# Attention in a two-layer model: both parts of V in one operand, head norms token by token, forget gate in two passes

## The chip, the cores and the metric

The kernel runs on one core of a Trainium2 chip. The metric is the device time of one execution in microseconds. Five engines work side by side, each through its own instructions in a fixed order: TensorE (PE, whose weight loads have a row of their own in the profile, PEld), VectorE (DVE), ScalarE (ACT), GpSimd (POOL), and SyncE (SP), which issues most of the transfers.

## The reference, cut to what matters

The model has two layers over 512 tokens of width 1024. Layer 0 mixes tokens with a gated linear recurrence, layer 1 with attention that has a forget gate (`fox_mixer`); each layer ends in a feed-forward part that retrieves 16 of 16384 experts per head. The change lies in the attention of layer 1 alone.

```python
def fox_mixer(h, in_w, f_b, q_norm_g, k_norm_g, out_w):
    q, k, v, f_logit, og = jnp.split(h @ in_w, [D, 2 * D, 3 * D, 3 * D + H], axis=-1)
    q = rms_norm(q.reshape(B, S, H, E), q_norm_g)          # 16 heads of 64
    k = rms_norm(k.reshape(B, S, H, E), k_norm_g)
    log_f = jax.nn.log_sigmoid(f_logit + f_b)
    cum = jnp.cumsum(log_f, axis=1)                        # per head
    ...
        s = einsum(q, k) * scale + cum[query] - cum[key]   # causal
        p = jax.nn.softmax(s, axis=-1)
        o = einsum(p, v)
    o = o * jax.nn.sigmoid(og)
    return o @ out_w
```

`rms_norm` multiplies by 1/sqrt(mean of squares + 1e-6) over the 64 entries of a head. `h` is the normed and modulated input; `f_logit` is 16 columns wide, one for each head.

## The kernel before, in words

Everything is computed to nearly float32 from two rounded parts: a tensor x is kept as hi = round(x) and lo = x − hi in the type fp32r, and a product of two such tensors is three matmuls, hi·hi, hi·lo and lo·hi (L428 to L430 in `proj_t`; `split`, L229 and L230, makes the parts, the high one on ScalarE, the low one on VectorE).

The attention stage `fox` first computes V for all heads (`values`, in two halves of 512 columns), and between the halves the forget gate: one projection whose 128 columns hold the 16 gate columns and zeros (24 matmuls of 512 tokens), then log-sigmoid, a running sum `cum`, and eight writes of its parts to the DRAM tensor `cx` by GpSimd's queue. From there rows go into the tiles qx and kx, so that the score product adds cum[query] − cum[key] by itself.

Then come eight head pairs, each 128 rows (two heads of 64, called par 0 and par 1). For one pair:

- `heads_norm` projects q and k (2 × 24 matmuls of 512 tokens, L428 to L430). ScalarE makes the squares `sq` (L1215) and a scaled copy `raw` (L1217). A matmul with `sel` as weights (8 columns wide) streams the squares and sums them by head into `ssq`, 8 rows of 256 tokens (L1219). VectorE scales and inverts them (L1222, L1223), ScalarE takes the square root (L1224), which needs a table of its own, and `split` makes two parts rh and rl. Matmuls with `selT` as weights spread these over the 128 rows into `rsb` (L1233, L1234), and VectorE multiplies (L1235).
- `prepare` makes from them the operands qs, qx, ks and kx (L1262 to L1276), eight copies on ScalarE and four subtractions on VectorE.
- `attend` goes through four query blocks for each head: scores `s` by two matmuls (L1293, L1294), mask and maximum on VectorE, the exponential on ScalarE (L1300), reciprocal and scaling on VectorE, transposes `tp` of the probabilities (L1305), and `split` into pth and ptl. Then the product with V: for each of four key blocks three matmuls into `o`, with weights vh, vh and vl (L1310 to L1312). vh holds both heads of the pair, so half of the 128 output rows is the other head's and is not used. Last, `o` goes into y, for the first two pairs through VectorE together with the output gate (L1314), for the others by a copy on ScalarE (L1316).

The loop in the text prepares pairs 0 and 1 first, and pair j + 2 after pair j's attention. The order on each engine is made by the framework's scheduler ahead of time: it takes the earliest instruction in program order that its own estimate of times holds ready, so projections fill the places where the scores wait. On the chip each engine keeps that order whatever the real times are. `bg.pump` hands out rows of the next modulation (VectorE L195, their loads by GpSimd's queue) between the steps. The last six output gates are projected during the last two pairs. The PSUM tag "n" has one buffer, which ssq and rsb of all pairs share in turn.

## Time and profile before

| | us |
|---|---|
| median of 3 runs | 3116.62 |
| lowest, highest | 3116.06, 3117.3 |
| the profiled execution, its own time | 3118.31 |
| its span in the profile | 3116.5 |
| first ssq matmul to last matmul start of o, within the span | 1596.8 to 1819.3 |

The profile is one execution; the times in its views are microseconds from the start of its span. A group's row gives engine, operation, output and inputs, shapes and count, then busy time, the mean length of one in nanoseconds, and the idle time of the engine before them with what ended it. Ends of matmuls are modelled, starts are recorded. For a matmul "128*8 128x256" means weights of 128 rows and 8 columns, and 256 streamed columns; the input that is named first is the streamed one.

### The profile page before, as it was taken

To read this page: it belongs to the slowest core of one execution; us is meant where nothing else is said; L and a number is where in the kernel's file an instruction comes from. 1 tells how busy PE (TensorE), PEld (TensorE's weight loads), DVE (VectorE), ACT (ScalarE), POOL (GpSimd) and SP (SyncE) were. 2 spreads that over 40 slices of the span, in tenths; PEclk is the share of its full clock that TensorE was granted. 3 is DMA by queue.
4 is the path that set the end of the run, shared out by engine and by line. 5 is a ranking of instruction groups with operands and counts; after the bars stand their busy time and mean duration, and the time that the engine had idled before them with its cause. 6 is when DMAs were issued, how large, how long until landed. Compare 5 with 4: busy or idle time off the path is not lost.

```text
span 3116.5 us, 44537 instructions
## 1 busy us (share of the span) xinstructions
PE 3041.4 (98%) x16192; PEld 2672.8 (86%) x16192; DVE 2559.3 (82%) x5274; ACT 1468.3 (47%) x2131; POOL 958.0 (31%) x846
## 2 busy tenths in 40 slices
PE   7999999999999999999999999999999999999999
PEld 5877899988888888888777778999988888888888
DVE  7876889878988888888579867899869887888786
ACT  5754247873333333333457843267843333333332
POOL 0001430007654245452011003400046444444450
PEclk9999999999999999999999999999999999999999
DMA  7543245779999999998332123346699999999994
GB/s 271 170 173 122 102 152 204 269 296 398 403 381 369 349 366 362 375 355 300 131 120 83 56 105 107 126 159 245 257 370 398 349 362 346 354 344 351 340 330 162
DMA packets 300429, 818.99 MB, mean 263 GB/s; under 512 B 28848, under 2 KB 151728, under 8 KB 271664
## 3 DMA queue, kind: packets, MB, share of 16 engines
q1 hardware_dynamic: 168464, 388.79, 35.0%
q0 software_dynamic: 90272, 324.58, 27.6%
q10 hardware_dynamic: 41472, 102.78, 8.5%
q8 instruction: 127, 2.08, 0.3%
q14 instruction: 94, 0.77, 0.1%
HBM read 735.03 MB, written 81.02 MB: 262 GB/s over the span
## 4 chain that ended last, share of the span: by engine, by line
PE 68%; DVE 12%; DMA 6%; issue 3%; ACT 2%; POOL 1%; DVEq 0%; SPq 0%; POOLq 0%; ACTq 0%
PE vacc L1048 26%; PE pacc L428 10%; PE pacc L430 10%; PE pacc L429 10%; DVE wlo L230 3%; PE gps L909 2%; DMA wraw<-in_l_v_dram 2%; DMA wraw<-in_l_uT_dram 2%; DVE rows L957 1%; DVE ge L820 1%; DMA at<-ascr 1%; PE oacc L470 1%; PE oacc L471 1%; PE oacc L469 1%; DVE pg L933 1%
## 5 line engine op out<-in xcount | busy, mean ns | idle before, releaser
L229 ACT ACTIVATE whi<-wraw 128x1024 fp32r<-128x1024 f32 (+1 forms) x646 | 663.0, 1033 | 611.2 <-PE pacc L429 346.7
L428 PE MATMUL pacc<-hhi,whi 128*128 128x384 f32 (+1 forms) x2616 | 920.9, 352 | 13.1 <-ACT at L1028 6.8
L430 PE MATMUL pacc<-hhi,wlo 128*128 128x384 f32 (+1 forms) x2616 | 915.4, 350 | 7.5 <-DVE wlo L230 7.3
L429 PE MATMUL pacc<-hlo,whi 128*128 128x384 f32 (+1 forms) x2616 | 912.2, 349 | 0.0
L230 DVE TENSOR_TENSOR wlo<-wraw,whi 128x1024 fp32r<-128x1024 f32 (+1 forms) x580 | 699.9, 1211 | 212.3 <-ACT whi L229 204.7
L1048 PE MATMUL vacc<-whi,wl 128*128 128x512 f32 x1536 | 601.0, 391 | 2.3 <-DVE wl L1041 2.3
L1048 PE MATMUL vacc<-wlo,wh 128*128 128x512 f32 x1536 | 600.7, 391 | 0.8 <-DVE wlo L230 0.8
L1048 PE MATMUL vacc<-whi,wh 128*128 128x512 f32 x1536 | 598.2, 389 | 0.3 <-ACT whi L229 0.3
L428 PEld LDWEIGHTS pacc<-hhi,whi 128*128 128x128 f32 x2616 | 492.2, 188 | 45.1 <-ACT at L1028 7.8
L430 PEld LDWEIGHTS pacc<-hhi,wlo 128*128 128x128 f32 x2616 | 491.6, 188 | 36.6 <-DVE wlo L230 12.0
L429 PEld LDWEIGHTS pacc<-hlo,whi 128*128 128x128 f32 x2616 | 492.1, 188 | 28.6 <-issue 1.7
L1038 ACT ACTIVATE wh<-at 128x384 fp32r<-128x384 f32 x256 | 134.1, 525 | 778.4 <-DVE at L1034 489.2
L948 POOL DMA_INDIRECT rows<-in_l_v_dram,ei x256 | 355.6, 1389 | 360.6 <-DVE accg L972 335.5
L948 POOL DMA_INDIRECT rows<-in_l_u_dram,ei x256 | 368.7, 1440 | 263.4 <-DVE rows L957 208.9
L1048 PEld LDWEIGHTS vacc<-whi,wl 128*128 128x128 f32 x1536 | 288.7, 188 | 63.4 <-DVE wl L1041 2.6
L1048 PEld LDWEIGHTS vacc<-wlo,wh 128*128 128x128 f32 x1536 | 288.7, 188 | 58.7 <-DVE wlo L230 1.1
L1048 PEld LDWEIGHTS vacc<-whi,wh 128*128 128x128 f32 x1536 | 288.7, 188 | 57.7 <-ACT whi L229 0.7
L972 DVE SCALAR_TENSOR_TENSOR accg<-rows,act,accg 128x1024 f32<-128x1024 f32 x254 | 324.8, 1279 | 0.5
L957 DVE SCALAR_TENSOR_TENSOR rows<-rows,hn 128x1024 f32<-128x1024 f32 x256 | 305.0, 1218 | 7.7 <-DMA rows<-in_l_u_dram,ei 7.3
L1034 DVE TENSOR_TENSOR at<-at,gtile 128x384 f32<-128x384 f32 x256 | 140.9, 552 | 125.3 <-DMA at<-ascr 122.3
L911 ACT ACTIVATE st<-gps 128x512 f32<-128x512 f32 x192 | 186.8, 1112 | 33.6 <-PE gps L909 33.4
L230 POOL TENSOR_TENSOR wlo<-wraw,whi 128x1024 fp32r<-128x1024 f32 (+1 forms) x66 | 134.4, 2048 | 188.4 <-ACT whi L229 188.4
(297 smaller groups left out, 3371.4 us busy)
## 6 DMA issues: line engine op xcount, KB each, us to landing
wraw<-in_l_uT_dram SPq DMA_DIRECT2D x128, 1024.0 KB
wraw<-in_l_v_dram SPq DMA_DIRECT2D x128, 1024.0 KB
gscr<-st ACTq DMA_DIRECT2D x48, 1024.0 KB
gtile<-gscr SPq DMA_DIRECT2D x90, 512.0 KB
mw<-in_l_ffn_mw_dram POOLq DMA_DIRECT2D x48, 512.0 KB
...
```

The source lines that it names most:

```text
L229: g.nc.scalar.activation(hi, raw, AF.Copy)
L230: (eng or g.nc.vector).tensor_sub(lo, raw, hi)
L428: nc.tensor.matmul(ps, whi[:, k, :], hhi[:, k, :n], start=(k == 0), stop=False)
L429: nc.tensor.matmul(ps, whi[:, k, :], hlo[:, k, :n], start=False, stop=False)
L430: nc.tensor.matmul(ps, wlo[:, k, :], hhi[:, k, :n], start=False, stop=(k == KD - 1))
L911: A.activation(st[:, :, q * 4:q * 4 + 4].rearrange("p e t -> p t e"), gps, AF.Copy, scale=1.0 / GSCALE)
L948: i = nc.gpsimd.indirect_dma_start(out=rows, out_offset=None, in_=src, in_offset=bass.IndirectOffsetOnAxis(ap=ei[:, j:j + 1], axis=0))
L957: V.scalar_tensor_tensor(r, r, 1.0, hn, op0=OP.mult, op1=OP.mult, accum_out=act[:, j:j + 1]))
L972: tc.keep_in_program_order(V.scalar_tensor_tensor(acc, r, w, acc, op0=OP.mult, op1=OP.add))
L1034: pin(V.tensor_tensor(at.rearrange("p (b t) -> p b t", t=16), at.rearrange("p (b t) -> p b t", t=16), gts[c // 8][:, :, c % 8, :], op=OP.m ...
L1038: pin(A.activation(wh, at, AF.Copy))
L1048: T.matmul(acc[t][d], x[:, ts], y[:, d, :], start=(i == 0 and x is wh and y is vh), stop=(i == PK - 1 and x is wl))
```

## The change

It has three parts.

1. *V.* The tile `vs` holds for each key block four parts of 64 columns: high of head 0, low of head 0, low of head 1, high of head 1. A head's weights are two neighbouring parts, so one matmul gives the product with the high part in one half of the output rows and with the low part in the other half. Two matmuls per key block remain, one for pth and one for ptl (the product of two low parts, left out before, is now included). ScalarE copies the half with the low part across into `ol`, VectorE adds the two halves.
2. *Head norms.* The squares become the weights (128 × 128, four token blocks) and `sel`, now two columns, is streamed: the sums stand token by token, 128 rows of 16. VectorE scales them, GpSimd raises them to −0.5, and reciprocal, square root and split are gone. ScalarE spreads each value over 64 columns (`wide`), and TensorE transposes `wide` into `rsb`. `heads_norm` is cut in two, `sums` and `spread`; `prepare` becomes `stacked`. `attend` is now a generator that stops after each head: between the two heads of pair j, pair j + 1 is spread and stacked, and the sums of pair j + 2 are made.
3. *Forget gate.* The 16 gate columns stand twice among the 128 weight columns, at 0 and at FS = 32. VectorE copies the low part of the second set into the high operand, which then carries both parts, and 16 matmuls do. ScalarE takes the second set with the bias, VectorE adds the first.

```diff
@@ -22,7 +22,7 @@
 EPS = 1e-6
 FH = 16
 FE = 64
-NU = 2
+FS = 32
 LATE = 2
 PH = 8
 PK = 128
@@ -1159,22 +1159,25 @@
             V.tensor_scalar(qgc, qgc, FE ** -0.5, None, op0=OP.mult)
             fbc = fp.tile([FH, 1], F32, name="fbc")
             nc.sync.dma_start(fbc, fb)
-            sel = fp.tile([128, 2, NU, NU * 4], F32, name="sel")
+            sel = fp.tile([128, 2], F32, name="sel")
             V.memset(sel, 0.0)
-            for u in range(NU):
-                for i in range(2):
-                    for hd in range(2):
-                        r = u * 4 + i * 2 + hd
-                        V.memset(sel[hd * 64:hd * 64 + 64, i, u, r:r + 1], 1.0)
-            selT = fp.tile([NU * 4, 2, NU, 128], F32R, name="selT")
+            for hd in range(2):
+                V.memset(sel[hd * FE:hd * FE + FE, hd:hd + 1], 1.0)
             mask = fp.tile([128, 128], F32, name="mask")
             V.tensor_scalar(mask, offsets(g, g.work), 0.5, -1.0e30, op0=OP.is_gt, op1=OP.mult)
             with pool(tc, name="foxf", bufs=1) as ff, \
                     pool(tc, name="fps0", bufs=1, space=PSUM) as psum:
                 values(0, order[2:], psum, ws)
-                ps = proj_t(g, psum, h)
+                whi, wlo = g.stream.take()
+                V.tensor_copy(whi[:, :, FS:FS + FH], wlo[:, :, FS:FS + FH])
+                ps = psum.tile([128, S], F32, name="pacc", tag="acc")
+                for k in range(KD):
+                    for i, x in enumerate(h):
+                        T.matmul(ps, whi[:, k, :], x[:, k, :], start=(k == 0 and i == 0), stop=(k == KD - 1 and i == 1))
+                zl = ff.tile([FH, S], F32, name="zl")
+                A.activation(zl, ps[FS:FS + FH], AF.Identity, bias=fbc)
                 z = ff.tile([FH, S], F32, name="z")
-                A.activation(z, ps[:FH], AF.Identity, bias=fbc)
+                V.tensor_add(z, zl, ps[:FH])
                 lf = log_sigmoid(g, ff, z, FH)
                 one = ff.tile([FH, S], F32, name="one")
                 V.tensor_tensor(one, z, z, op=OP.is_equal)
@@ -1192,11 +1195,6 @@
                 for side, rows in enumerate(((oner, oner, ch, cl), (nch, ncl, oner, oner))):
                     for i, r in enumerate(rows):
                         tc.keep_in_program_order(nc.gpsimd.dma_start(cx[:, side, i, :], r))
-                for i in range(2):
-                    for u in range(NU):
-                        ps = psum.tile([128, 128], F32, name="selps", tag="selps", bufs=2)[:NU * 4]
-                        T.transpose(ps, sel[:, i, u, :], g.ident)
-                        A.activation(selT[:, i, u, :], ps, AF.Copy)
                 ws = []
                 values(1, order[:2], eps, ws)
                 values(1, order[2:], psum, ws)
@@ -1204,10 +1202,9 @@
             with pool(tc, name="foxw", bufs=2) as fw, \
                     pool(tc, name="fps", bufs=2, space=PSUM) as psum:
 
-                def heads_norm(parts):
-
-                    n = S // NU
-                    ss = psum.tile([NU * 4, n], F32, name="ssq", tag="n", bufs=1)
+                def sums(parts):
+
+                    ss = psum.tile([128, TC, 2, 2], F32, name="ssq", tag="n", bufs=1)
                     raw = []
                     for i, gc in enumerate(parts):
                         ps = proj_t(g, psum, h)
@@ -1215,26 +1212,28 @@
                         A.activation(sq, ps, AF.Square)
                         r = fw.tile([128, S], F32, name="raw", tag=f"raw{i}")
                         A.activation(r, ps, AF.Copy, scale=gc)
-                        for u in range(NU):
-                            T.matmul(ss, sel[:, i, u, :], sq[:, u * n:(u + 1) * n], start=(i == 0 and u == 0),
-                                     stop=(i == 1 and u == NU - 1))
+                        for t in range(TC):
+                            T.matmul(ss[:, t, i, :], sq[:, t * 128:t * 128 + 128], sel, start=True, stop=True)
                         raw.append(r)
-                    V.tensor_scalar(ss, ss, 1.0 / FE, EPS, op0=OP.mult, op1=OP.add)
-                    V.reciprocal(ss, ss)
-                    A.activation(ss, ss, AF.Sqrt)
-                    rh = fw.tile([NU * 4, n], F32R, name="rh", tag="rh", bufs=1)
-                    rl = fw.tile([NU * 4, n], F32R, name="rl", tag="rl", bufs=1)
-                    split(g, rh, rl, ss)
-                    out = []
+                    n = TC * 4
+                    rs = fw.tile([128, 4 * n], F32, name="rs", tag="rs")
+                    V.tensor_scalar(rs[:, :n], ss.rearrange("p a b c -> p (a b c)"), 1.0 / FE, EPS,
+                                    op0=OP.mult, op1=OP.add)
+                    nc.gpsimd.tensor_tensor(rs[:, n:2 * n], rs[:, :n], g.mhalf.to_broadcast([128, n]), op=OP.pow)
+                    return raw, rs[:, n:2 * n].rearrange("p (a b c) -> p a b c", b=2, c=2)
+
+                def spread(raw, rs):
+
                     for i, r in enumerate(raw):
+                        wide = fw.tile([128, S], F32, name="wide", tag="wide", bufs=1)
+                        A.activation(wide.rearrange("p (t a b) -> p t a b", a=2, b=FE),
+                                     rs[:, :, i, :].unsqueeze(3).to_broadcast([128, TC, 2, FE]), AF.Copy)
                         b = psum.tile([128, S], F32, name="rsb", tag="n", bufs=1)
-                        for u in range(NU):
-                            us = slice(u * n, (u + 1) * n)
-                            T.matmul(b[:, us], selT[:, i, u, :], rh, start=True, stop=False)
-                            T.matmul(b[:, us], selT[:, i, u, :], rl, start=False, stop=True)
+                        for t in range(TC):
+                            ts = slice(t * 128, t * 128 + 128)
+                            T.transpose(b[:, ts], wide[:, ts], g.ident)
                         V.tensor_mul(r, r, b)
-                        out.append(r)
-                    return out
+                    return raw
 
                 def gate(j):
 
@@ -1250,8 +1249,8 @@
                 for j in range(LATE):
                     gate(j)
                     bg.pump(1.2)
-                def prepare(j):
-                    qn, kn = heads_norm((qgc, kgc))
+                def stacked(j, raw, rs):
+                    qn, kn = spread(raw, rs)
                     stacks = []
                     for par in range(2):
                         own = slice(par * 64, par * 64 + 64)
@@ -1278,11 +1277,12 @@
                     return stacks
 
                 def attend(j, stacks):
-                    vh = fw.tile([128, TC, 128], F32R, name="vh", tag="vh")
-                    vl = fw.tile([128, TC, 128], F32R, name="vl", tag="vl")
-                    split(g, vh, vl, vt[:, :, j * 128:(j + 1) * 128])
+                    vs = fw.tile([128, TC, 4, FE], F32R, name="vs", tag="vs")
+                    split(g, vs[:, :, 0:4:3], vs[:, :, 1:3],
+                          vt[:, :, j * 128:(j + 1) * 128].rearrange("p t (a b) -> p t a b", b=FE))
                     for par in range(2):
                         own = slice(par * 64, par * 64 + 64)
+                        oth = slice(64 - par * 64, 128 - par * 64)
                         qs, qx, ks, kx = stacks[par]
                         pth = fw.tile([128, TC, S], F32R, name="pth", tag="pth", bufs=1)
                         ptl = fw.tile([128, TC, S], F32R, name="ptl", tag="ptl", bufs=1)
@@ -1307,24 +1307,34 @@
                         o = psum.tile([128, S], F32, name="o", tag="o", bufs=1)
                         for kb in range(TC):
                             qsl = slice(kb * 128, S)
-                            T.matmul(o[:, qsl], vh[:, kb, :], pth[:, kb, qsl], start=(kb == 0), stop=False)
-                            T.matmul(o[:, qsl], vh[:, kb, :], ptl[:, kb, qsl], start=False, stop=False)
-                            T.matmul(o[:, qsl], vl[:, kb, :], pth[:, kb, qsl], start=False, stop=(kb == TC - 1))
+                            w = vs[:, kb, par * 2:par * 2 + 2, :].rearrange("p a b -> p (a b)")
+                            T.matmul(o[:, qsl], w, pth[:, kb, qsl], start=(kb == 0), stop=False)
+                            T.matmul(o[:, qsl], w, ptl[:, kb, qsl], start=False, stop=(kb == TC - 1))
+                        ol = fw.tile([128, S], F32, name="ol", tag="ol", bufs=1)
+                        A.activation(ol[own], o[oth], AF.Copy)
                         if j < LATE:
-                            V.scalar_tensor_tensor(y[own, j, :], y[own, j, :], 1.0, o[own], op0=OP.add, op1=OP.mult)
+                            V.tensor_add(ol[own], ol[own], o[own])
+                            V.scalar_tensor_tensor(y[own, j, :], y[own, j, :], 1.0, ol[own], op0=OP.add, op1=OP.mult)
                         else:
-                            A.activation(y[own, j, :], o[own], AF.Copy)
+                            V.tensor_add(y[own, j, :], ol[own], o[own])
                         bg.pump(1.2)
-
-                ready = [prepare(0)]
+                        yield
+
+                gains = (qgc, kgc)
+                ready = stacked(0, *sums(gains))
                 bg.pump(1.2)
-                ready.append(prepare(1))
+                due = sums(gains)
+                bg.pump(1.2)
                 for j in range(KD):
-                    attend(j, ready[j])
+                    heads = attend(j, ready)
+                    next(heads)
+                    if j + 1 < KD:
+                        ready = stacked(j + 1, *due)
                     if j + 2 < KD:
-                        ready.append(prepare(j + 2))
+                        due = sums(gains)
                         bg.pump(1.2)
-                    else:
+                    next(heads)
+                    if j + 2 >= KD:
                         bg.finish()
                         n = (KD - LATE) // 2
                         for i in range(LATE + (j + 2 - KD) * n, LATE + (j + 3 - KD) * n):
@@ -1444,7 +1454,8 @@
     o["fox_qk"] = pairs(blocks(w[:, 0:D]), blocks(w[:, D:2 * D]))
     o["fox_v"] = halves(w[:, 2 * D:3 * D])
     wf = np.zeros((D, 128), np.float32)
-    wf[:, :FH] = w[:, 3 * D:3 * D + FH]
+    for i in (0, FS):
+        wf[:, i:i + FH] = w[:, 3 * D:3 * D + FH]
     o["fox_f"] = blocks(wf)[0]
     o["fox_og"] = blocks(w[:, 3 * D + FH:])
     o["fox_fb"] = C(f["l1_fox_f_b"][:, None])
```

The order on TensorE, at the product with V of one head (o is the output, pth and ptl the two parts of the transposed probabilities as streamed operand, vh, vl and vs the weights). Before:

```order
L1310 MATMUL o<-pth,vh 128x512
L1293 MATMUL s<-ks,qs 128x512
L1294 MATMUL s<-kx,qx 128x512
L428 MATMUL pacc<-hhi,whi 128x512
L429 MATMUL pacc<-hlo,whi 128x512
L1311 MATMUL o<-ptl,vh 128x512
L1312 MATMUL o<-pth,vl 128x512
L1310 MATMUL o<-pth,vh 128x384
L1311 MATMUL o<-ptl,vh 128x384
L1312 MATMUL o<-pth,vl 128x384
```

In the changed kernel, the same head of the same pair:

```order
L1312 MATMUL o<-ptl,vs 128x512
L1311 MATMUL o<-pth,vs 128x384
L1312 MATMUL o<-ptl,vs 128x384
L1311 MATMUL o<-pth,vs 128x256
L1312 MATMUL o<-ptl,vs 128x256
L1311 MATMUL o<-pth,vs 128x128
L1312 MATMUL o<-ptl,vs 128x128
```

Of three rows for each length two are left.

The order on TensorE again, from the last sums of pair 2 (ssq) to the first broadcast of that pair (rsb). Before, what follows the sums:

```order
L1219 MATMUL ssq<-sq,sel 8x256 x2
L1293 MATMUL s<-ks,qs 128x128
L1294 MATMUL s<-kx,qx 128x128
L430 MATMUL pacc<-hhi,wlo 128x512
L1293 MATMUL s<-ks,qs 128x256
L1294 MATMUL s<-kx,qx 128x256
```

and in the changed kernel:

```order
L1216 MATMUL ssq<-sel,sq 128x2 x4
L429 MATMUL pacc<-hlo,whi 128x512
L430 MATMUL pacc<-hhi,wlo 128x512
L428 MATMUL pacc<-hhi,whi 128x512
L429 MATMUL pacc<-hlo,whi 128x512
L430 MATMUL pacc<-hhi,wlo 128x512
L428 MATMUL pacc<-hhi,whi 128x512
L1234 MATMUL rsb<-ident,wide 128x128 x3
```

Before, 37 rows stand between them; now six projections do.

The order on ScalarE at the same norm of pair 2. Before:

```order
L1224 ACT_TABLE_LOAD
L1224 ACTIVATE ssq<-ssq 8x256
L229 ACTIVATE rh<-ssq 8x256
L1300 ACT_TABLE_LOAD
L1300 ACTIVATE p,l<-s,nm 128x128
```

and in the changed kernel:

```order
L1229 ACTIVATE wide<-rs 128x512
L1300 ACTIVATE p,l<-s,nm 128x128
L1229 ACTIVATE wide<-rs 128x512
L1300 ACTIVATE p,l<-s,nm 128x256
```

The table loads around the root are gone from the attention, and the exponentials of the running pair now stand behind `wide`, which takes its values from GpSimd.

## The prediction

> **What bounds the kernel now.** I read the page's busy times first, then the stretches of the attention, then TensorE's own timeline. The page gives TensorE 98%:
>
> ```profile
> PE 3041.4 (98%) x16192; PEld 2672.8 (86%) x16192; DVE 2559.3 (82%) x5274; ACT 1468.3 (47%) x2131; POOL 958.0 (31%) x846
> ```
>
> A share over the whole program says nothing about the changed stage, so here are four stretches of it (length; busy us of PE, weight loads, VectorE, ScalarE, GpSimd; granted clock; DMA):
>
> ```profile
> 1600.00:1650.00 50.00, 49.57 (x236) 36.16 (x235) 38.54 (x80) 38.81 (x72) 3.08 (x6) 1.00 0.21 67
> 1650.00:1700.00 50.00, 49.76 (x247) 37.25 (x245) 46.31 (x116) 40.64 (x81) 6.77 (x13) 1.00 0.29 105
> 1700.00:1750.00 50.00, 49.70 (x254) 36.91 (x253) 43.50 (x107) 42.51 (x91) 4.97 (x10) 1.00 0.14 44
> 1750.00:1800.00 50.00, 49.31 (x255) 37.78 (x254) 44.89 (x115) 39.89 (x91) 2.05 (x5) 1.00 0.17 55
> ```
>
> PE is full, but its ends are modelled. The starts settle it: if each matmul starts one stream length after the one before, PE sets the time. TensorE's timeline of one head pair (start, length, operation, count):
>
> ```profile
> 1711.98 1.03 PE L1219 MATMUL ssq<-sq,sel 128*8 128x256 f32 x4
> 1712.94 0.50 PE L428 MATMUL pacc<-hhi,whi 128*128 128x512 f32 x1
> ...
> 1717.79 0.93 PE L1305 MATMUL tp<-ident,p 128*128 128x128 f32 x7
> 1718.47 0.48 PE L430 MATMUL pacc<-hhi,wlo 128*128 128x512 f32 x1
> ...
> 1721.14 0.39 PE L1312 MATMUL o<-pth,vl 128*128 128x512 f32 x1
> 1721.36 0.34 PE L1310 MATMUL o<-pth,vh 128*128 128x384 f32 x1
> ...
> 1721.71 0.34 PE L1312 MATMUL o<-pth,vl 128*128 128x384 f32 x1
> 1721.88 0.28 PE L1310 MATMUL o<-pth,vh 128*128 128x256 f32 x1
> ...
> 1722.12 0.28 PE L1312 MATMUL o<-pth,vl 128*128 128x256 f32 x1
> 1722.24 0.22 PE L1310 MATMUL o<-pth,vh 128*128 128x128 f32 x1
> ...
> 1722.41 0.27 PE L1312 MATMUL o<-pth,vl 128*128 128x128 f32 x1
> 1722.52 0.51 PE L1305 MATMUL tp<-ident,p 128*128 128x128 f32 x3
> ...
> 1723.79 0.38 PE L1233 MATMUL rsb<-rh,selT 8*128 8x256 f32 x1
> ...
> 1724.46 0.50 PE L430 MATMUL pacc<-hhi,wlo 128*128 128x512 f32 x1
> ...
> 1731.71 0.40 PE L429 MATMUL pacc<-hlo,whi 128*128 128x512 f32 x1
> 1732.40 0.50 PE L1310 MATMUL o<-pth,vh 128*128 128x512 f32 x1 [0.30 <-ACT pth L229]
> ...
> 1736.67 0.60 PE L1219 MATMUL ssq<-sq,sel 128*8 128x256 f32 x2
> ```
>
> Start to start, a matmul of 512 columns takes 0.22, of 384 0.17, of 256 0.12, of 128 0.11, a transpose of 128 columns 0.68/7 = 0.097, four rows of ssq 0.96, four of rsb 0.67. One pair takes 1736.67 − 1711.98 = 24.69 us, and the one real wait in it is 0.69 − 0.22 = 0.47 us at 1732.40. So what is taken off TensorE here comes off the time, as long as VectorE and ScalarE follow: they stand at 43.31 and 40.46 of 50 on the mean of the four stretches. The clock is 1.00 throughout.
>
> **The change part by part, on TensorE.** *V's two parts in one operand.* Per head and key block three products become two: the L1312 row goes. 16 heads × (0.22 + 0.17 + 0.12 + 0.11) = **−9.9**. *Forget gate.* 24 products of 512 columns become 16: 8 × 0.22 = **−1.8**. The added VectorE copy of the low part stands long before its first product, under the products of V; the added ScalarE and VectorE steps end in cx, whose last write starts at 1582.1 and whose readers start at 1616.9, so 35 us of projections hide them (about 1 us if that cover is gone):
>
> ```profile
> L1194 POOL DMA_DIRECT2D cx<-oner x4: 484/490/582, 1560.6 to 1582.1; - x4
> ...
> L1294 PE MATMUL s<-kx,qx x64: 272/331/477, 1616.9 to 1810.1; 68*128 68x128 f32 x16, 68*128 68x256 f32 x16, 68*128 68x384 f32 x16, 68*128 68x512 f32 x16
> ```
>
> *selT.* Four transposes go: **−0.4**. *Broadcast of the norm.* Sixteen groups of four rsb products (0.67) become sixteen of four transposes (4 × 0.097 = 0.39): **−4.5**. The order splits some of these groups, but the count of places where TensorE goes from one operand kind to another is 168 in both orders, so I add nothing.
>
> *Sums of squares.* This is the operation that the trace doesn't show: 64 products with squares as the 128-column weights and two streamed columns. The order lists two rows of ssq where the timeline has four, so each is two records: 128 records for sixteen groups of 0.96 = 15.4 us. From below they could cost nothing (−15.4). From above each waits for a whole weight load:
>
> ```profile
> L1048 PEld LDWEIGHTS vacc<-whi,wl 128*128 128x128 f32 x1536 | 288.7, 188 | 63.4 <-DVE wl L1041 2.6
> ```
>
> 128 × 0.188 = 24.1 (+8.7). I take the transpose's 0.097, the nearest row, since it too loads 128 × 128 of plain f32 each time: 12.4, so **−3.0**. Sum on TensorE: **−19.6**, between −32 and −7.9.
>
> The Trainium skill, "TensorE: Matmul & The Clock Gate" (Part 3, "What overlaps and what doesn't"), says that a weight load overlaps a running matmul only if the row group differs. By that rule the new records would queue load behind load, which is the upper price above. The trace disagrees for full-height operands: 0.188 us loads vanish under products that start 0.22 us apart.
>
> **On the other engines.** Durations in this stage (group | busy, mean ns | idle before):
>
> ```profile
> L1224 ACT ACT_TABLE_LOAD x8 | 10.3, 1283 | 0.1
> L1300 ACT ACT_TABLE_LOAD x8 | 10.3, 1283 | 0.1
> L1224 ACT ACTIVATE ssq<-ssq 8x256 f32<-8x256 f32 x8 | 2.7, 334 | 1.8 <-DVE ssq L1223 1.6
> L229 ACT ACTIVATE rh<-ssq 8x256 fp32r<-8x256 f32 x8 | 2.9, 359 | 0.0
> L229 ACT ACTIVATE vh<-vt 128x512 fp32r<-128x512 f32 x8 | 4.9, 627 | 1.4 <-PE o L1311 1.4
> L1316 ACT ACTIVATE y<-o 64x512 f32<-64x512 f32 x12 | 7.1, 588 | 5.2 <-PE o L1312 5.0
> ```
>
> ```profile
> L1223 DVE RECIPROCAL ssq<-ssq 8x256 f32<-8x256 f32 x8 | 13.9, 1743 | 0.0
> L1222 DVE TENSOR_SCALAR ssq<-ssq 8x256 f32<-8x256 f32 x8 | 3.3, 410 | 0.5 <-PE ssq L1219 0.5
> L230 DVE TENSOR_TENSOR rl<-ssq,rh 8x256 fp32r<-8x256 f32 x8 | 3.2, 405 | 2.8 <-ACT rh L229 2.8
> L1263 DVE TENSOR_TENSOR qs<-raw,qs 64x512 fp32r<-64x512 f32 x16 | 11.0, 686 | 0.5
> ```
>
> ScalarE, per pair: two table loads, the root and rh go (2.57 + 0.33 + 0.36 = 3.26), two wide copies come (2 × 0.63); ol replaces y at the same 0.59. 40.46/50 × 24.69 = 20.0 becomes 18.0. VectorE: 1.74 + 0.41 + 0.41 = 2.56 go; two adds of 0.69 and a small scaling of about 0.2 (estimated from L1222) come: 43.31/50 × 24.69 = 21.4 becomes 20.4. TensorE's pair becomes 24.69 − 2×0.62 − 2×0.28 − 2×0.18 = 22.5. So both still fit below it, VectorE at 91%; but in 1650:1700, where the modulation rows run, 46.3 − 2.0 against 50 − 4.4 is 97%. I charge **+3** for waits of in-order engines run so close (none at best; 4 pairs × 2.2 = 8.6 if VectorE lets no gain through in the first four).
>
> *The new wait: GpSimd's power.* It stands between the last ssq row and the first rsb transpose: TensorE finishes the group (0.8 + 0.2), VectorE scales (0.2), GpSimd, ScalarE spreads (0.63), and some 0.3 of hand-overs, the small ones estimated: 2.1 + P. ScalarE's wide row holds up the exponentials queued behind it, and TensorE the projections behind rsb. What the new order leaves between those two rows, counted with the starts above: 2.5, 4.1, 2.3, 6.2, 12.1, 8.6, 7.1, 8.0 us for pairs 0 to 7. For P, a power of 128×16, the trace has 128×1 (min/median/max) and plain GpSimd work of two sizes:
>
> ```profile
> L349 POOL TENSOR_TENSOR rs<-ms,mhalf x16: 542/549/1582, 9.4 to 1871.8; 128x1 f32<-128x1 f32 x16
> L230 POOL TENSOR_TENSOR wlo<-wraw,whi 128x1024 fp32r<-128x1024 f32 x52 | 124.5, 2401 | 176.9 <-ACT whi L229 176.9
> L230 POOL TENSOR_TENSOR wlo<-wraw,whi 128x256 fp32r<-128x256 f32 x14 | 10.3, 738 | 11.5 <-ACT whi L229 11.5
> ```
>
> From below 0.55, all of it start-up. From above 16 × 0.549 = 8.8. A subtraction costs (2401 − 738)/768 = 2.2 ns per element, so its start-up is 0.18 and a power of one element 0.37 more, part of it call and part arithmetic. I take P = 1.3 (about 50 ns per element, twenty times a subtraction): 3.4 is needed, and pairs 0 and 2 miss by 0.9 and 1.1: **+2**. The skill's "GPSIMD Engine Reference" (§3.1) has about 2.6 cycles per element for a two-input add, worked out at its 1.2 GHz an estimate of 0.58 us here, by which this wait would be 0.6 us in all; the subtraction's 2.2 ns agrees with it, but no run here shows a power of that width.
>
> *The end.* The last two heads' transposes now stand right before their PV products, with no projection between: about 0.6 for pth, as the y row, then part of ptl. **+1**.
>
> **Sum.** −19.6 + 3 + 2 + 1 = −13.6. The profiled execution took 3118.31 (span 3116.5), so it becomes 3104.7; the runs' median, 3116.62, lies 1.7 lower: **3103.0 us**.
>
> **The rivals.** *A, the power is priced per element (slower).* P = 8.8 makes 10.9 against the slack above: 8.4 + 6.8 + 8.6 + 4.7 + 0 + 2.3 + 3.8 + 2.9 = 37.5 instead of 2, so 3116.6 + 21.9 = 3138.5. It decides from P = 5.4 on, where the misses reach 15.6. For it: one element already takes three times a subtraction's start-up. Against it: a start-up of a longer routine would look the same. 12%. *B, VectorE takes over.* It does 20.4 of work per pair and keeps the 3.3 of waits it has now: 23.7, so only 1 us per pair is gained, 8 in all, with 2.2 from forget gate and selT and 3 lost: 3109.4. For it: 97% in one stretch. Against it: its waits today are waits for a full TensorE. 15%, half of it on either side of the bound. *C, weight loads show.* ssq costs +8.7 instead of −3.0: 3114.7, no change. The overlapped loads speak against it. 8%. *D, the tiny products start twice as fast* as the transposes: 3103.0 − 6.2 = 3096.8. Nothing in the trace shows a start below 0.097 after a full f32 load. 7%.
>
> **Chances and range.** The forecast (3097 to 3110) has 58%. A measurement of this kernel tells 0.2% (6 us) from no change. Faster: 58 + 7 + half of B, 73%. Same: C and the other half of B, 15%. Slower: A, 12%. The range from 3096 to 3118 leaves out A and a little below; the forecast's own is 3097 to 3110.
>
> **What would show it.** No table loads between the first and last exponential of the attention; a pair of about 22.5 us of starts; three records of 512 to two in o; 128 ssq records starting about 0.1 apart; a power of 1 to 2 us and TensorE's waits at rsb in pairs 0 and 2 alone. It is wrong if the power takes over 5 us, if ssq starts lie 0.19 apart, or if VectorE shows no idle time and PE does.

## The result, and the profile after

| | before | after |
|---|---|---|
| median of six runs each, us | 3116.97 | 3136.0 |
| lowest, highest | 3116.06, 3122.21 | 3130.67, 3139.24 |
| the profiled execution, its own time | 3118.31 | 3136.13 |
| its span | 3116.5 | 3134.3 |

The ratio of the times is 1.0053 [1.0041, 1.0065] (in brackets the 95% interval): the change makes the kernel slower by half a per cent, 17 us by the ratio and 19 by the two medians, where 13.6 us less were forecast.

TensorE is a point less busy. The page of the changed kernel, part 1 (busy us, share of the span, instructions):

```profile
PE 3033.2 (97%) x16180; PEld 2680.8 (86%) x16180; DVE 2554.0 (81%) x5270; ACT 1457.2 (46%) x2116; POOL 987.0 (31%) x854
```

The four stretches of the attention that the prediction showed of before, now of the changed kernel (length; busy us of PE, weight loads, VectorE, ScalarE, GpSimd; granted clock; DMA):

```profile
1600.00:1650.00 50.00, 43.24 (x222) 34.68 (x221) 31.59 (x72) 32.08 (x60) 16.64 (x16) 0.97 0.31 107
1650.00:1700.00 50.00, 45.16 (x245) 36.19 (x243) 42.27 (x108) 34.69 (x77) 9.56 (x12) 1.00 0.14 48
1700.00:1750.00 50.00, 45.08 (x240) 35.77 (x240) 39.52 (x103) 38.25 (x85) 9.84 (x11) 0.97 0.09 30
1750.00:1800.00 50.00, 44.12 (x222) 35.74 (x221) 37.60 (x102) 35.58 (x80) 7.92 (x8) 0.90 0.11 33
```

TensorE, full before, has 5 to 7 us of gaps in each 50, VectorE and ScalarE are emptier too, and the clock is below 1.00 in three of the four. So no engine is the bound: they wait for one another, and the clock falls. The view of TensorE's waits names whom it waits for (total us, times, longest), from V's first product to the output projection's first; the three largest groups:

```profile
PE rsb L1234 <- ACT wide L1229: 15.6, 7, 2.6
PE s L1293 <- ACT p L1300: 5.2, 5, 2.8
PE o L1311 <- ACT pth L229: 2.1, 3, 1.1
```

Over half of it stands at the broadcast, behind `wide`. The instructions on the tile rs give the chain ahead of that (min/median/max ns, first and last start), and below them who waited for rows on this tile (us, times):

```profile
L1220 DVE TENSOR_SCALAR rs<-ssq x8: 165/170/176, 1602.3 to 1776.8; 128x16 f32<-128x16 f32 x8
L1222 POOL TENSOR_TENSOR rs<-rs,mhalf x8: 2912/2922/3827, 1602.6 to 1777.0; 128x16 f32<-128x16 f32 x8
...
  POOL rs L1222: 45.9, 8
  ACT wide L1229: 28.1, 8
```

The power of 128×16 takes 2.92 us; the prediction took 1.3. With the 0.55 of one column that makes 0.158 us for each further column; the run with two powers of 8 columns, below, tests it.

But a longer power alone does not explain it. In pair 5 the prediction counted 8.6 us between the last sum and the first broadcast, more than the 2.1 + 2.92 that are needed, and TensorE waits there all the same. The changed kernel's timeline of that place, a row or two from each engine:

```profile
1716.68 0.95 PE L1216 MATMUL ssq<-sel,sq 128*128 128x2 f32 x8
1721.53 1.22 DVE L230 TENSOR_TENSOR wlo<-wraw,whi 128x1024 fp32r<-128x1024 f32 x1
...
1723.26 1.22 DVE L230 TENSOR_TENSOR wlo<-wraw,whi 128x1024 fp32r<-128x1024 f32 x1
1724.39 0.17 DVE L1220 TENSOR_SCALAR rs<-ssq 128x16 f32<-128x16 f32 x1
1724.65 2.92 POOL L1222 TENSOR_TENSOR rs<-rs,mhalf 128x16 f32<-128x16 f32 x1 [7.00 <-DVE rs L1220]
1727.59 0.63 ACT L1229 ACTIVATE wide<-rs 128x512 f32<-128x512 f32 x1 [2.12 <-POOL rs L1222]
1728.28 0.44 PE L1234 MATMUL rsb<-ident,wide 128*128 128x128 f32 x2 [1.99 <-ACT wide L1229]
```

The last sum's group begins at 1716.68 and takes under 1 us, but VectorE's scaling of 0.17 us stands so late in VectorE's own fixed order that it starts at 1724.39; the rows ahead of it follow each other without a gap. Some seven of the 8.6 us go by before GpSimd is let on.

The pairs differ in this. In pairs 0 to 2 the scaling follows the last sums at once (1602.31, 1619.44 and 1638.95, each 1.1 to 1.2 us after that group's start), and the waits of 2.22, 1.49 and 2.51 us come from the length of the power. In pairs 3 to 6 it starts 5.6 to 13.2 us after the last group (1667.59, 1698.43, 1724.39, 1748.64), and the waits are 2.56, 2.32, 1.99 and 2.47 us. In pair 7 it is late too (6.6 us), and nobody waits.

The third part is the clock. Around the wait of pair 2, first the timeline (start, length), then stretches of 2 us:

```profile
1642.85 0.90 PE L1234 MATMUL rsb<-ident,wide 128*128 128x128 f32 x3 [2.51 <-ACT wide L1229]
...
1645.25 0.63 PE L428 MATMUL pacc<-hhi,whi 128*128 128x512 f32 x1
1645.68 0.63 PE L429 MATMUL pacc<-hlo,whi 128*128 128x512 f32 x1
```

```profile
1642.00:1644.00 2.00, 1.15 (x5) 1.16 (x6) 0.83 (x3) 0.98 (x3) 0.13 (x1) 0.70 0.84 324
1644.00:1646.00 2.00, 2.00 (x7) 1.61 (x6) 1.31 (x6) 1.08 (x3) 0.59 (x1) 0.50 0.36 152
1646.00:1648.00 2.00, 2.00 (x10) 1.50 (x10) 0.79 (x5) 0.28 (x1) 0.23 (x1) 0.95 0.67 246
```

After the wait the granted clock is 0.50 for about 3.4 us, and products of 512 columns start 0.43 us apart instead of 0.23.

**An account of the stage.** From these views the stage can be added up, the same way for every kernel below. Its length goes from the start of V's first product (the first vacc row with hhi) to that of the first oacc product, the output projection. Waits are the waits that TensorE's timeline marks with a releaser between these two starts. Lost clock is the sum over stretches of 2 us of (1 − granted clock) × 2. What remains of the difference to before, once waits and lost clock are taken off, is put down to TensorE's own work. (Half clock during a wait is in both sums, which makes the rest come out too low: by 0.3 us in the changed kernel, by up to 3 us in those below.) Before: 1528.1 to 1821.4, 293.3 us, waits 2.9, no lost clock. After: 1528.7 to 1837.3, 308.6 us (+15.3), waits 27.3 (+24.4), lost clock 10.2, so the rest is −19.3. The forecast for TensorE's work was −19.6: that term holds, and some 35 us of waits and clock stand against it.

### The profile page after: what moved, and what is told of

It reads as the page before. It is cut to its first block, busy times and chain, and to the rows that moved or that the text cites. A ratio compares the mean times of both kernels' runs of the same rounds, so it can differ in the third digit from the quotient of the medians.

```text
span 3134.3 us, 44509 instructions
## 1 busy us (share of the span) xinstructions
PE 3033.2 (97%) x16180; PEld 2680.8 (86%) x16180; DVE 2554.0 (81%) x5270; ACT 1457.2 (46%) x2116; POOL 987.0 (31%) x854
## 5 line engine op out<-in xcount | busy, mean ns | idle before, releaser
L428 PE MATMUL pacc<-hhi,whi 128*128 128x384 f32 (+1 forms) x2608 | 921.4, 353 | 10.3 <-ACT at L1028 6.8
L430 PE MATMUL pacc<-hhi,wlo 128*128 128x384 f32 (+1 forms) x2608 | 915.4, 351 | 12.6 <-DVE wlo L230 12.3
L948 POOL DMA_INDIRECT rows<-in_l_u_dram,ei x256 | 375.5, 1467 | 255.9 <-DVE rows L957 199.8
```

The costliest lines, as they stand in the source:

```text
L428: nc.tensor.matmul(ps, whi[:, k, :], hhi[:, k, :n], start=(k == 0), stop=False)
L430: nc.tensor.matmul(ps, wlo[:, k, :], hhi[:, k, :n], start=False, stop=(k == KD - 1))
L948: i = nc.gpsimd.indirect_dma_start(out=rows, out_offset=None, in_=src, in_offset=bass.IndirectOffsetOnAxis(ap=ei[:, j:j + 1], axis=0))
```

## The experiments

All times are medians, each ratio to runs of the kernel before on the same chip; its medians there were 3119.4 to 3121.4. Stage, waits and clock come from one profiled execution each; they stand together in the table at the end.

### The three parts alone

V and forget gate, with the norms and the loop of before. The hunks are those of the change on vs, o and the forget gate; but here ol has no buffer of its own: for the first two pairs it shares that of the squares, and for the others the copy goes straight into y:

```diff
-ol = fw.tile([128, S], F32, name="ol", tag="ol", bufs=1)
+ol = fw.tile([128, S], F32, name="ol", tag="sq", bufs=1) if j < LATE else y[:, j, :]
```

> The kernel before with two of the three parts of the change: V's two parts in one operand and the forget gate in two passes; the head norms and the loop over pairs are those of before. (ol has no buffer of its own here: for pairs 2 to 7 ScalarE copies straight into y, for pairs 0 and 1 into the buffer of sq.) Theory 1 (the loss comes from the new head norms: the chain of VectorE's scaling, GpSimd's power and ScalarE's spreading, for which TensorE waits some 2.4 us in each pair, and a clock that falls with these waits): -9.9 for V and -1.8 for the gate, about 1 lost at the end, 3106 us, granted clock 1.00 from 1600 to 1800. Theory 2 (V's half copied across and added makes the heads wait on each other): no gain, 3115 us or more.

Measured: 3143.89 us, 1.0073 [1.0049, 1.0097], as theory 2 had it. The part that was to take the most work from TensorE costs 23 us. So the norms are not the only trouble.

The norms alone, with the new loop, V and forget gate as before:

> The changed kernel with only the head norms token by token and their loop; V and the forget gate are those of before. Theory 1: the changed kernel's 3136 plus the 11 us that V and gate save, about 3147 us; waits of 2 to 3 us at rsb in every pair, clock under 1.00. Theory 2: TensorE's saving of 7.9 for the norms is there and nothing else, about 3109 us.

Measured: 3135.38 us, 1.0059 [1.0039, 1.008]; stage +12.7, 12.7 us of waits at the broadcast alone: the waits of theory 1, and a time between the two forecasts.

The forget gate alone:

> The kernel before with the forget gate in two passes alone: eight products fewer, 8 x 0.22 = 1.8 us. Theory (V's part makes the waits of the kernel that had V's and the gate's part): 3114 to 3119, same as before within 0.2%, clock 1.00 in the stage. Rival (the longer chain behind the gate's projection, or another order that follows from it, makes them): 3135 to 3147.

Measured: 3121.11 us, 0.9996 [0.9985, 1.0006]; its stage is 1.7 us shorter, no wait added. It does what was forecast for its work (−1.8), and is innocent; the kernel before took 3121.4 on this chip.

V alone, with ol as above:

> The kernel before with V's two parts in one operand alone: TensorE has 9.9 us less work. Theory (with fewer products behind which to hide, VectorE's and ScalarE's chain of a softmax block, still with its table loads, sets the time in the first pairs): 3138 to 3147, as with the forget gate added (3143.89), waits of 3 to 5 us ahead of transposes of the probabilities and clock below 0.9 in 1650 to 1700. Rival (the saving comes off): 3105 to 3110, with the clock at 1.00.

Measured: 3140.42 us, 1.0066 [1.005, 1.0083]. V's part by itself is what costs in the first kernel. The time is the theory's; its reason, too few products to hide behind, falls with the next run. Its timeline at the first long wait (PE, then VectorE, then ScalarE):

```profile
1646.79 0.87 PE L1306 MATMUL tp<-ident,p 128*128 128x128 f32 x3 [4.43 <-DVE p L1303]
...
1642.51 0.68 DVE L1317 TENSOR_TENSOR ol<-ol,o 64x512 f32<-64x512 f32 x1 [1.17 <-ACT ol L1315]
1643.32 0.67 DVE L1318 SCALAR_TENSOR_TENSOR y<-y,ol 64x512 f32<-64x512 f32 x1
1643.92 1.21 DVE L195 SCALAR_TENSOR_TENSOR mw<-mw,sc 128x1024 f32<-128x1024 f32 x1
1645.59 0.66 DVE L1298 TENSOR_REDUCE nm<-s 128x1 f32<-128x512 f32 x1
...
1641.89 0.59 ACT L1315 ACTIVATE ol<-o 64x512 f32<-64x512 f32 x1
1646.28 0.69 ACT L1301 ACTIVATE p<-s,nm 128x512 f32<-128x512 f32 x1 [3.40 <-DVE nm L1298]
```

What I call the fold (copy of o by ScalarE, sum of the halves and y by VectorE) waits for the product with V to end. Behind it in VectorE's fixed order stand a modulation row of 1.21 us and the maximum of the next softmax block, behind that the exponential, behind that TensorE's transposes: a wait of 4.43 us. Of the 20.3 us of waits in the stage, 14 lie before 1690, in the first two pairs, where the fold has two steps on VectorE and the borrowed buffer. The view of the tile sq names no wait for ol or y, so the buffer itself does not show as what is waited for.

### The fold, taken away

V alone as above, but y written from o as before (for the first two pairs by VectorE's step of before, L1314 there); the low part of V is left out:

```diff
-A.activation(ol[own], o[oth], AF.Copy)
-V.tensor_add(y[own, j, :], ol[own], o[own])
+A.activation(y[own, j, :], o[own], AF.Copy)
```

> The kernel before with V's two parts in one operand alone, but without the fold: the half of o with the low part is not copied and not added, y is written straight from o as before. It leaves the low part of V out. Theory (what turned V's saving of 9.9 us into a loss of 20 is the fold: ScalarE's copy of o and VectorE's one or two steps of 0.69 us stand in both engines' fixed orders ahead of the next softmax block, so that block starts only after the product with V): 3103 to 3112, no wait of TensorE over 2 us between 1630 and 1700, clock 1.00. Rival (fewer products cover the softmax chain less, whatever becomes of o): 3128 to 3142, with waits of 3 to 5 us at the transposes of the probabilities as in the kernel with the fold.

Measured: 3119.69 us, 0.9999 [0.9984, 1.0013]. The 20 us are gone, so the fold makes the loss here. The price holds for this kernel, where for two pairs it also shares its buffer with the squares. The gain that theory wanted on top does not come either: its stage is 2.2 us shorter, with 8.3 us of waits, of which 5.5 are for exponentials. TensorE's rest is −9.2, so the products are saved (9.9 were forecast) and mostly waited away.

The same in the whole changed kernel, with the low part of V left out:

> The changed kernel without the fold: y is written straight from o, the low part of V is left out. Theory (here TensorE waits for the power first, 15.6 of 26.6 us of waits, and the fold stands in its shade): 3124 to 3136. Rival (the fold costs here what it costs with V's part alone, 20 us): 3110 to 3119.

Measured: 3130.54 us, 1.0031 [1.0021, 1.0042], as the theory had it. Its stage is 7.6 us shorter than with the fold, and its waits at the broadcast grow:

```profile
PE rsb L1234 <- ACT wide L1229: 18.3, 8, 2.5
```

The waits elsewhere fall from 11.7 us to 6.1 (before: 2.9).

### The power

The changed kernel without the power; the norm is left out, the scaled sums are used as they are:

```diff
-V.tensor_scalar(rs[:, :n], ss.rearrange("p a b c -> p (a b c)"), 1.0 / FE, EPS,
+V.tensor_scalar(rs[:, n:2 * n], ss.rearrange("p a b c -> p (a b c)"), 1.0 / FE, EPS,
                 op0=OP.mult, op1=OP.add)
-nc.gpsimd.tensor_tensor(rs[:, n:2 * n], rs[:, :n], g.mhalf.to_broadcast([128, n]), op=OP.pow)
```

> The changed kernel without GpSimd's power: VectorE's scaled mean square goes straight to ScalarE's spreading, so q and k are multiplied by the mean square, not by its root's inverse (that part of the computation is left out). Same products, transposes, copies and adds. Theory 1: the waits at rsb shrink from about 17 us in all to under 5, the granted clock is 1.00 in nearly all of the attention, 3102 to 3110 us. Theory 3 (the clock falls by itself, since the two-column products and the transposes keep TensorE too little busy, waits or not): clock still 0.90 to 0.97 in stretches of the attention, over 3115 us.

Measured: 3107.75 us, 0.996 [0.9946, 0.9974], as theory 1 had it, with 0.1 us of lost clock; theory 3, a clock that falls without the waits, fails here. This is the only kernel here that is clearly faster than before. Its waits, the three largest groups, none at the broadcast among them:

```profile
PE s L1292 <- ACT p L1299: 3.2, 7, 1.5
PE o L1310 <- ACT pth L229: 2.1, 3, 1.1
PE oacc L469 <- ACT yhi L229: 1.4, 1, 1.4
```

All of V's part and the fold are in it, and the stage is 11.9 us shorter. So the power turns the change from a gain into a loss: 28 us between this kernel and the changed one, while the eight powers last 23.4. (The text differs in the power alone, but the fixed orders are made anew for every kernel, this one too.)

The sums of q and of k scaled and raised apart, 8 columns each instead of 16 at once (the same for the scaling on VectorE):

```diff
-    n = TC * 4
+    n = TC * 2
...
-nc.gpsimd.tensor_tensor(rs[:, n:2 * n], rs[:, :n], g.mhalf.to_broadcast([128, n]), op=OP.pow)
+    for i, gc in enumerate(parts):
+        nc.gpsimd.tensor_tensor(rs[:, w], rs[:, u], g.mhalf.to_broadcast([128, n]), op=OP.pow)
```

> The changed kernel with the sums of q and of k scaled and raised apart: two powers of 128x8 per pair instead of one of 128x16. By the power's 2.92 us for 16 columns and 0.55 for one, one of 8 columns takes 0.55 + 7 x 0.158 = 1.65 us, and q's lies under k's 24 projections (5.4 us). Theory (the waits behind the power, and the half clock that follows them, ate TensorE's saving): the waits at the first broadcast of a pair fall from 2.4 us to below 1 us, the clock stays at 1.00 for most of the stage, and the time comes to 3105 to 3118, between the kernel without the power (3107.75) and before. Rival (any order in which the norms are made between the two heads of a pair loses as much, whatever the power takes): 3128 to 3140, as for the changed kernel and the one with the sums first.

Measured: 3124.63 us, 1.0016 [1.0003, 1.0029]. The price by width came as worked out:

```profile
L1224 POOL TENSOR_TENSOR rs<-rs,mhalf x16: 1623/1663/2715, 1597.3 to 1764.8; 128x8 f32<-128x8 f32 x16
```

The wait at the broadcast falls from 15.6 us to 1.0, but the time stays above the range of 3105 to 3118: 15.8 us of waits are left, now for pth (5.1), p and the squares, and 3.4 us of clock.

Root on ScalarE as before, on 128×16:

```diff
-nc.gpsimd.tensor_tensor(rs[:, n:2 * n], rs[:, :n], g.mhalf.to_broadcast([128, n]), op=OP.pow)
+V.reciprocal(rs[:, :n], rs[:, :n])
+A.activation(rs[:, n:2 * n], rs[:, :n], AF.Sqrt)
```

> The changed kernel with the inverse root of 128x16 by VectorE's reciprocal and ScalarE's square root, as before, in place of GpSimd's power. ScalarE gets two table loads of 1.28 us per pair again, the first of which can run while it waits for the sums. Theory (the length of the power is what counts): the chain gets shorter by 2.92 - 0.17 - 0.3 = 2.4 us per pair, or by 1.2 where the table load stands in it, 10 to 19 us in all: 3115 to 3127. Rival (ScalarE's fixed order is the narrow place: the root and its table loads hold up the exponentials as long as the power did): 3130 to 3145.

Measured: 3120.76 us, 0.9984 [0.9968, 0.9999]. That is the theory's range. With the table loads back, it is some 0.7% below the changed kernel by the two ratios, and level with before or a touch faster.

### The order

The sums of pair j + 2 ahead of the spreading of pair j + 1, and those of pair 1 ahead of the spreading of pair 0:

```diff
-ready = stacked(j + 1, *due)
+own = due
 due = sums(gains)
+ready = stacked(j + 1, *own)
```

> The changed kernel with one swap in program order: between the two heads of pair j the sums of pair j + 2 are made first and only then is pair j + 1 spread and stacked (and at the start the sums of pairs 0 and 1 before pair 0 is spread). The power still takes 2.9 us, but has a whole pair to do it. Theory 1: waits at rsb gone or under 5 us in all, clock 1.00, 3102 to 3110 us. Theory 3: clock still below 1.00, over 3115 us. If the power itself disturbs the others (its 23 us in all, on the memory that VectorE uses too): 3115 to 3125 us with no waits at rsb.

Measured: 3129.45 us, 1.0042 [1.0025, 1.006]. The waits at the broadcast go, but 13.2 us of waits stand elsewhere (5.3 for p), and the lost clock is 13.6. No forecast had the time; a clock below 1.00 was theory 3's. Nor does the power visibly slow VectorE beside it: in the changed kernel the sum into y (L1319) takes 0.68 us at 1725.51, under a power, and 0.69 at 1718.04, without one.

The loop of before around the operations of the changed kernel:

```diff
-heads = attend(j, ready)
-next(heads)
-ready = stacked(j + 1, *due)
-due = sums(gains)
-next(heads)
+for _ in attend(j, ready[j]):
+    pass
+ready.append(stacked(j + 2, *sums(gains)))
```

> The changed kernel with the loop of before: pair j + 2 is summed, spread and stacked in one piece after pair j's attention. All operations are those of the changed kernel. Theory (the new loop lays the power bare; in the old one the chain of norms, 3.4 us long then, cost TensorE no wait at all): under 6 us of waits at the broadcast, 3108 to 3122. Rival (the power is too long for any of these orders): 10 us or more of waits at the broadcast, 3128 to 3142.

Measured: 3126.83 us, 1.0023 [1.0012, 1.0034], between the two forecasts, with the rival's waits at the broadcast:

```profile
PE rsb L1234 <- ACT wide L1229: 10.2, 8, 2.2
```

So the new loop costs about 9 of the 15 us that the stage grew by, and the power is too long for the old loop as well.

The fold written after the second query block of the next head, with two powers; it becomes a function that is kept until then:

```diff
+folds.append(fold)
...
+if qb == 1 and folds:
+    folds.pop()()
```

> The kernel with two powers of 128x8 per pair, and each head's fold (copy of o, sum of the two halves, y) written after the second query block of the next head instead of right behind its product with V. Theory (the fold in the way of the next softmax blocks is most of what is left): 3108 to 3118, at most a third of the waits over 0.6 us left. Rival (the fold only changes places and still stands in the order before some block): 3120 to 3130, as with two powers alone (3124.63).

Measured: 3124.13 us, 1.0004 [0.9992, 1.0017]; stage 296.1 against 295.6 of the kernel with two powers alone. The rival's answer.

### Looking for what keeps the saving

New norms with two powers and two-pass forget gate, V as before:

> The kernel with the new norms and the forget gate in two passes, two powers of 128x8 per pair, and V as before (three products, no fold). TensorE has 9.9 us more work than in the kernel with two powers and V in one operand (3124.63). Theory (the fold costs more than the products it saves): 3108 to 3120, faster than that one. Rival (with the power halved, V's saving comes off): 3125 to 3135.

Measured: 3125.51 us, 1.0004 [0.999, 1.0017]: level with before, inside the rival's range. By the ratios (1.0004 here, 1.0016 with V in one operand) it is no slower than the kernel with 9.9 us less work, and that little apart they decide nothing between the two.

The same with the root on ScalarE instead of two powers, in the new loop:

> New norms with VectorE's reciprocal and ScalarE's square root in place of the power, forget gate in two passes, V as before (three products, no fold), the new loop. TensorE has 1.8 + 0.4 + 4.5 + 3.0 = 9.7 us less work than before. Theory (fold and power were what lost the saving): stage from V's first product to o's last at 280 to 287 us (before 291.2), time 3110 to 3117, faster than before by 0.2% or more. Rival (any shortening of TensorE's work lays bare the chain of the softmax, and waits and half clock take it back): level with before, 3118 to 3126.

Measured: 3121.88 us, 1.0003 [0.9992, 1.0015]. The stage was forecast only to o's last product, 284.4 us in the profile and so in the range; but six gates are projected after that, and to the output projection it is 1.7 us shorter than before. The rival's time.

And in the loop of before:

> As the one with the root and V as before, but in the loop of before. Theory (the old loop keeps more rows between sums and broadcast): 3108 to 3115, waits in the stage under 5 us. Rival (the loop makes no difference): within 3 us of the one in the new loop.

Measured: 3117.86 us, 0.9991 [0.9978, 1.0005]. The stage is 5.7 us shorter, with 6.2 us of waits; the time shows 0.1%, which can't be told from nothing, and is 4 us below the new loop, between the two forecasts.

V in one operand added to that (root, old loop, whole change otherwise):

> The changed kernel (V in one operand, forget gate in two passes, norms token by token) with VectorE's reciprocal and ScalarE's root in place of the power, and the loop of before. Theory (with the short chain and the old loop, waits fall to a few us, and the fold costs less than V's 9.9 us): stage 283 to 290 us to the first product of the output projection (before 293.3, V as before 287.6), time 3106 to 3116. Rival (the fold costs as much as it saves): 3116 to 3125, level with V as before.

Measured: 3119.83 us, 1.0004 [0.9991, 1.0017], the rival. Against the one above, TensorE's rest is −19.5 instead of −10.7, and 7.0 us more of waits and 11.4 more of lost clock make its stage 9.6 us longer. No version that computes the whole norm beats before by more than 0.2%.

### The clock

Eight useless products of 512 columns ahead of each pair's first broadcast:

```diff
+for t in range(8 if i == 0 else 0):
+    T.matmul(b, hhi[:, t % KD, :128], hhi[:, t % KD, :], start=True, stop=True)
```

> The changed kernel with eight useless products of 512 columns put before the first broadcast of each pair, into the same PSUM tile, which the broadcast then writes over: 64 more products, 64 x 0.23 = 14.7 us more work for TensorE at the very place where it waits 2.4 us per pair. Theory (what costs beside the waits themselves is the half clock that follows them, 11.9 us between 1580 and 1850): TensorE is no longer idle there, the work fits in the waits, and the lost clock mostly goes: 3120 to 3132, faster than the changed kernel in spite of more work, with under 6 us of clock lost. Rival (the clock falls by itself or by the length of the stage): the lost clock stays at 10 us or more, and the time is 3136 to 3150.

Measured: 3142.96 us, 1.0078 [1.0061, 1.0095]. In the profile (which took 3133.6) the lost clock falls to 1.7 us as the theory said, but waits of 20.7 remain, now for p (6.6) and the squares (4.4), so the useless work is not hidden. The time is the rival's. It settles nothing on the clock, since the products changed the order too.

So the clock was tried by itself: three waits put into the kernel before, among V's products, where nothing else waits.

```diff
+def stall(psum, n):
+    T.transpose(d, g.ident, g.ident)
+    V.tensor_scalar(x[:, 0, :n], d[:, :n], 1.0, 2.0, op0=OP.mult, op1=OP.add)
+    nc.gpsimd.tensor_tensor(x[:, 1, :n], x[:, 0, :n], g.mhalf.to_broadcast([128, n]), op=OP.pow)
+    T.transpose(e[:n], x[:, 1, :n], g.ident)
```

> The kernel before with three useless chains put among the products of V, where TensorE otherwise waits for nothing between 1530 and 1600 and its clock is 1.00: a transpose, a scaling on VectorE, a power of 128x24, 128x16 or 128x8 on GpSimd, and a transpose of the result on TensorE a few products later. The powers take 0.55 + 0.158 per further column: 4.2, 2.9 and 1.65 us, so TensorE waits some 4.0, 1.5 to 2.5 and 1 us. Theory (a wait of over 2 us brings the half clock on): a stretch of 0.50 of 4 us or more begins within 3 us of the end of the first wait, perhaps of the second, none behind the third; 8 us of waits and 2 to 5 us of lost clock between 1530 and 1610. Rival (the half clock has another cause, as the number of changes between operations): clock 1.00 throughout that stretch.

Measured: 3129.93 us, 1.0044 [1.0028, 1.006]. The three waits, and a product behind the first, in the timeline:

```profile
1548.64 0.28 PE L1141 MATMUL ste<-ident,stx 128*24 128x128 f32 x1 [3.88 <-POOL stx L1139]
...
1550.37 0.63 PE L1157 MATMUL vacc<-whi,hhi 128*128 128x512 f32 x1
...
1571.58 0.28 PE L1141 MATMUL ste<-ident,stx 128*16 128x128 f32 x1 [3.06 <-POOL stx L1139]
...
1583.84 0.27 PE L1141 MATMUL ste<-ident,stx 128*8 128x128 f32 x1 [1.63 <-POOL stx L1139]
```

Stretches of 2 us behind the first and the second wait:

```profile
1550.00:1552.00 2.00, 2.00 (x6) 1.58 (x5) 0.00 (x0) 0.12 (x1) 0.00 (x0) 0.50 0.00 0
1552.00:1554.00 2.00, 2.00 (x7) 1.55 (x6) 1.03 (x1) 0.94 (x1) 0.00 (x0) 0.67 0.00 0
...
1572.00:1574.00 2.00, 2.00 (x11) 1.64 (x10) 1.90 (x4) 0.00 (x0) 0.00 (x0) 1.00 0.00 0
```

The wait of 3.88 us brings the half clock on, 1.2 us after its end and for 3.4 us (1549.88 to 1553.30); those of 3.06 and 1.63 us do not. The added waits, 8.6 us, and the lost clock, 1.7, make 10.3; the time grew by 10.5. So a wait can halve the clock, and the rival falls, since the second and the third wait bring the same operations with them. The theory's 2 us is no limit, since 3.06 us did not do it; its length of the stretch (4 us or more) was a little high. Where a wait falls matters too; the last section comes back to it.

### All kernels in one table

"Rest" is the stage's difference to before less the differences of waits and clock, to be read against TensorE's forecast work in the last column (by the prediction's terms: V −9.9, gate −1.8, norms −7.9; useless products +14.7; six transposes of the three waits +0.6).

| kernel | time, us | ratio | stage | waits | lost clock | rest | forecast work |
|---|---|---|---|---|---|---|---|
| before | 3116.97 | | 293.3 | 2.9 | 0 | | |
| after | 3136.0 | 1.0053 | 308.6 | 27.3 | 10.2 | −19.3 | −19.6 |
| V and gate | 3143.89 | 1.0073 | 310.4 | 20.4 | 14.0 | −14.4 | −11.7 |
| V alone | 3140.42 | 1.0066 | 314.0 | 20.3 | 15.6 | −12.3 | −9.9 |
| V alone, no fold | 3119.69 | 0.9999 | 291.2 | 8.3 | 1.7 | −9.2 | −9.9 |
| gate alone | 3121.11 | 0.9996 | 291.6 | 2.9 | 0.2 | −1.9 | −1.8 |
| norms alone | 3135.38 | 1.0059 | 306.0 | 19.4 | 3.4 | −7.3 | −7.9 |
| no power | 3107.75 | 0.996 | 281.4 | 9.7 | 0.1 | −18.8 | −19.6 |
| no fold | 3130.54 | 1.0031 | 301.0 | 24.4 | 6.8 | −20.6 | −19.6 |
| two powers | 3124.63 | 1.0016 | 295.6 | 15.8 | 3.4 | −13.9 | −19.6 |
| two powers, late fold | 3124.13 | 1.0004 | 296.1 | 16.1 | 5.7 | −16.1 | −19.6 |
| sums first | 3129.45 | 1.0042 | 298.5 | 13.2 | 13.6 | −18.8 | −19.6 |
| old loop | 3126.83 | 1.0023 | 299.6 | 21.7 | 9.2 | −21.6 | −19.6 |
| root | 3120.76 | 0.9984 | 294.1 | 14.2 | 11.0 | −21.4 | −19.6 |
| root, old loop | 3119.83 | 1.0004 | 297.2 | 13.2 | 13.1 | −19.5 | −19.6 |
| two powers, old V | 3125.51 | 1.0004 | 296.0 | 10.7 | 3.5 | −8.6 | −9.7 |
| root, old V | 3121.88 | 1.0003 | 291.6 | 6.0 | 6.8 | −11.7 | −9.7 |
| root, old V, old loop | 3117.86 | 0.9991 | 287.6 | 6.2 | 1.7 | −10.7 | −9.7 |
| useless products | 3142.96 | 1.0078 | 311.7 | 20.7 | 1.7 | −1.1 | −4.9 |
| three waits | 3129.93 | 1.0044 | 304.7 | 11.5 | 1.7 | 1.1 | 0.6 |

In all kernels but three the rest lies within 3 us of the forecast work (the 2.4 and 2.7 us of V alone and of V and gate are half clock during waits, counted twice). The exceptions are two powers, −13.9 for −19.6, two powers with the late fold, −16.1 for −19.6, and the useless products, −1.1 for −4.9. Idle time without a mark does not make it: with two powers TensorE is idle for 17.2 us of the stage, and 15.8 of them are marked. It stays open. The stage is one execution's, and the time holds scatter from outside it: the profile of before enters the stage at 1528.1, the one with two powers and old V at 1536.8, the one with the late fold at 1540.9, and up to this stage the text of the kernels is the same. So stage and time agree in direction, not to the microsecond.

## Why the prediction was wrong

**Right.** TensorE's sum: −19.6 forecast, −19.3 in the account. The 128 sums start about 0.1 us apart, not 0.19 (a group of eight takes 0.81 us from its start at 1716.68), so rivals C and D fall. Of the 16 table loads around the root and behind it one is left (at L1300), and VectorE did not become the bound (rival B): it has 8 to 18 us idle in each of the four stretches. The +1 at the end came to 1.5: the waits behind 1830 are 0.21, 1.06, 0.39 and 1.39 us, and 1.53 in the kernel before.

**Wrong: the price of the power.** P was taken as 1.3 of bounds 0.55 and 8.8; it is 2.92. The prediction read 0.37 us of the one-column power as "part of it call and part arithmetic" and gave the arithmetic 50 ns per element; it is 158. Rival A had the right mechanism (a price per element) at too high a size, 549 ns, and a point of decision, 5.4 us, that was too high too, for the next reason. That its 3138.5 comes near the measured 3136.0 is luck: it had 37.5 us of waits at the broadcast, and there are 15.6; other waits and the clock make up the difference.

**Wrong: the slack.** "What the new order leaves between those two rows, counted with the starts above" counted TensorE's rows alone. With P = 2.92, 5.0 us are needed, and that list would give misses of 2.5 + 0.9 + 2.7 = 6.1 us in pairs 0 to 2 and none later: still a gain. In pairs 0 to 2 that is what came, 6.2 us. But the trace has 15.6 us at the broadcast: the other 9.3 stand in pairs 3 to 6, where the list leaves room and VectorE's scaling starts late, in pair 5 (shown above) because of VectorE's own order. The slack of a chain over four engines has to be read in the order of each. Without the power the same loop costs no wait at the broadcast, and the loop of before costs 10.2 instead of 15.6.

**Wrong: +3 for waits of engines run close.** Beside the broadcast, 8.8 us of waits were added, 1.5 of them at the end. The fold is most of that: without it the waits there are 5.6 us less and the changed kernel's stage 7.6 us shorter. The prediction priced its steps as VectorE's and ScalarE's busy time, and found room for them; it did not ask what is queued behind them. In the timeline of V alone both engines hold the next softmax block until the product with V is done.

**Wrong: the clock.** "The clock is 1.00 throughout" was true of before and was carried over to a kernel with waits in it. It cost 10.2 us in the stage. With these in place of the forecast's +3, +2 and +1 the sum is −19.3 + 15.6 + 8.8 + 10.2 = +15.3, what the stage grew by. That it closes proves nothing, since −19.3 is what was left over; that this remainder is so near the forecast −19.6 does speak for the account.

**Left open.** Whether TensorE's saving can be kept with the whole norm computed. With power and fold out of the way the stage does get 5.7 us shorter, and the time is 2 us below the kernel before on the same chip (3117.86 against 3120.0), less than its scatter.
